# Gates of the first 128 tokens through a DRAM table: GpSimd scatters them, the up projection multiplies them in

## The chip, the cores and the metric

The kernel runs on one core of a Trainium2 chip. Five engines work on their own instruction streams and meet only in semaphores: PE (TensorE, matmuls), DVE (VectorE), ACT (ScalarE), POOL (GpSimd) and SP (SyncE, which here only issues DMAs). Times are microseconds of the device. The metric is the time of one execution, as the median of several runs.

## The reference, cut to what matters

Two blocks are computed one after the other on 256 tokens of 1024 features. The first has a spatial gating, a causal attention of 6 heads, a memory attention of 4 heads and a feed-forward part; the second has a state-space mixer, a convolution mixer and, last, a layer of 16384 small experts. In that last layer each token has 8 heads, and each head picks 16 experts out of 128 x 128 and gives each a gate:

```python
q1, q2 = jnp.split(q, 2, axis=-1)
s1 = jnp.einsum("thd,hkd->thk", q1, sub_keys_1)      # 128 scores per head
s2 = jnp.einsum("thd,hkd->thk", q2, sub_keys_2)
v1, i1 = lax.top_k(s1, 16); v2, i2 = lax.top_k(s2, 16)
cand = (v1[..., :, None] + v2[..., None, :]).reshape(t, 8, 256)
cand_idx = (i1[..., :, None] * 128 + i2[..., None, :]).reshape(t, 8, 256)
top_s, pos = lax.top_k(cand, 16)
expert_idx = jnp.take_along_axis(cand_idx, pos, axis=-1)
gate = jax.nn.softmax(top_s, axis=-1)
act = gelu(jnp.einsum("td,thkd->thk", x, w_down[expert_idx])) * gate
y = jnp.einsum("thk,thkd->td", act, w_up[expert_idx])
```

An expert that two heads of a token pick counts with the sum of its gates.

## The kernel before, in words

The kernel does not fetch single experts. It computes the activation of all 16384 experts for all 256 tokens and multiplies it by a table of gates that is zero where an expert was not picked. Matmuls that need full precision are done as three products of rounded parts: `load_split` loads a weight tile `wf` of 512 KB through SP, ACT rounds it to `wh` (L215), DVE subtracts to get `wl` (L216), and `mm3` (L220 to L222) multiplies. There are 4 buffers of `wf` and 3 of `wh` and `wl`.

Stages, in order of time in the trace of before: first block up to about 330 us, second block's mixers up to about 580 us, then the experts.

- **Mixers of the first block** (up to 120 us): six attention heads (`fox_head`, whose copy out of PSUM is L582) and four memory heads (`mem_head`, L669) run as background work beside projections. After the output projection the pool `ap` is closed and its memory goes to new tiles. Among them is `raw`, which POOL clears in part (L762) and SP then fills with 16 loads (L766); the weights of the feed-forward part stand behind these loads on SP.
- **Selection** (`select(t)`, one pass for each 128 tokens): DVE finds the 16 best of each head, then writes to `sl`, for each of the 128 tokens (partitions) and each of its 128 picks, the two halves i and j of the expert's index (the sums are L1331) and the gate (L1338). The second pass starts when the first is done. PE then transposes `sl` to `pj` (L1342), and ACT copies it to `jt`, in which a column is a token.
- **Down projection** (`for i in range(0, P, 2)`, 128 weight tiles `wd`): 24 matmuls per tile give `S`, expert pairs by 256 tokens; ACT writes its Gelu to the table `AT`, whose row i holds experts (i, j), j on the partitions. `AT` has 96 rows in one tile and 32 in another.
- **Gates** (`gates()`, background of the down projection, after both selections): for each of 256 tokens DVE builds a row of gates by i (`og`, L1407), ACT a row of ones by j (`oh`, L1409 and L1410), and PE multiplies the two (`pg`, L1414) to a table of 128 x 128. Four tokens are one step. Rows of `AT` that are there already are multiplied by `pg` (DVE, L1418); in the others `pg` is stored (ACT, L1421), and the row's Gelu is multiplied in later (ACT to `stage`, L1443; DVE, L1444).
- **Up projection** (`for i in range(P)`, 128 weight tiles `wu`): row i of `AT` is split to `ah` (ACT, L346) and `al` (DVE, L347), and 12 matmuls (L1470) add its product with `wu[i]` to four banks `acc`.

Background work is a generator that yields an estimated cost; `bg.run(budget)` after each weight tile lets it run on until the budget is used up. `BUDGET["select"]` holds until the first gates are there, `BUDGET["down"]` after it. The scheduler orders instructions by program order and priority; what is wrapped in `pin` keeps program order.

Of the kernel before, what the change touches and what calls it, by code (L numbers as in the profile page):

```python
# [16 lines left out]
P = 128  # L17
T = 256
# [17 lines left out]
for _n, _w in _ROWS:  # L36
# [9 lines left out]
    qk=1.5, kv=7.03, u=2.75, wo=2.51, diag=2.05,  # L46
    conf_c=0.995, xbc_c=1.4, conv=1.0,
    z=3.3, z_b=0.867, dt_wait=0.0575, ln_wait=6.66, wo2=3.32, wo2_b=5.58, gn_b=0.1,
    q=0.772, q_b=1.27, select=1.21, down=1.87,
)  # L50
FFN_WAIT, MIX_WAIT = 4.5, 5.5

# [104 lines left out]
def tile_two_blocks(ctx: ExitStack, tc: tile.TileContext, A, out):  # L157
# [172 lines left out]
    def pin(ins):  # L330
        tc.keep_in_program_order(ins)
# [210 lines left out]
    def softmax_t(name, sc, widths, addend):  # L542
# [20 lines left out]
            nc.tensor.transpose(sc[:, i * P:(i + 1) * P], S[:, i * P:(i + 1) * P], ident)  # L563
        yield 0.3

    pofs = {}

    def fox_head(h):
        hp, j = h // 2, h % 2
        pr = slice(64 * j, 64 * j + 64)  # L570
        while f"R{h}" not in done:
            yield None
        sc = bank(f"scf{h}")
        nc.tensor.matmul(sc[:, 0:P], qk[pr, hp, 0:P], qk[pr, 3 + hp, 0:P], start=True, stop=True,
                         skip_group_check=True)
        nc.tensor.matmul(sc[:, P:384], qk[pr, hp, P:T], qk[pr, 3 + hp, :], start=True, stop=True,
                         skip_group_check=True)
        yield 0.2
        yield from softmax_t(f"f{h}", sc, (P, T), R[:, h, :])

        PT = tp.tile([P, 512], F32, tag="PT", name=f"PTf{h}", bufs=3)
        nc.scalar.copy(PT[:, :384], sc[:, :384])  # L582
        yield 0.3
        if hp not in pofs:
            pofs[hp] = bank(f"pof{hp}")
        po = pofs[hp]
        nc.tensor.matmul(po[pr, 0:T], fv[:, 0, h * 64:h * 64 + 64], PT[:, 0:T], start=True, stop=False,
                         skip_group_check=True)
        nc.tensor.matmul(po[pr, P:T], fv[:, 1, h * 64:h * 64 + 64], PT[:, T:384], start=False, stop=True,
                         skip_group_check=True)  # L590
        yield 0.2
        split_to(oh[pr, 3 + hp, :], ol[pr, 3 + hp, :], po[pr, :T])
        yield 0.4
# [63 lines left out]
    def mem_head(h):  # L657
        hp, j = h // 2, h % 2
        pr = slice(64 * j, 64 * j + 64)
        sc = bank(f"scm{h}")  # L660
        for t in range(2):
            nc.tensor.matmul(sc[:, t * T:(t + 1) * T], qk[pr, 6 + hp, t * P:(t + 1) * P], kmT[pr, hp, :],
                             start=True, stop=True, skip_group_check=True)
        yield 0.2
        yield from softmax_t(f"m{h}", sc, (T, T), None)

        PT = tp.tile([P, 512], F32, tag="PT", name=f"PTm{h}", bufs=3)
        PT = PT.rearrange("p (m t) -> p m t", m=2)
        nc.scalar.copy(PT.rearrange("p m (t c) -> p t m c", t=2), sc.rearrange("p (t m c) -> p t m c", t=2, m=2))  # L669
        yield 0.3  # L670
        if hp not in poms:
            poms[hp] = bank(f"pom{hp}")
        po = poms[hp]
        for m in range(2):
            nc.tensor.matmul(po[pr, :T], vm[:, m, h * 64:h * 64 + 64], PT[:, m, :], start=(m == 0), stop=(m == 1),
                             skip_group_check=True)
        yield 0.2
        split_to(oh[pr, 6 + hp, :], ol[pr, 6 + hp, :], po[pr, :T])
        yield 0.4
# [30 lines left out]
    def add_normed(bs, gain, src, dst, eps, name, pool, tmp, then):  # L710

        with tc.high_priority(offset=PRIO):
# [27 lines left out]
                    then(m - 1)  # L740
            then(7)

    x1 = xp.tile([P, 8, T], F32, name="x1", tag="x1")
    h2h, h2l = act_pair("h2", T)
    add_normed(bs, "post_mix", x0, x1, eps1, "pm", xp, tp,
# [553 lines left out]

    ready = dict(q=0)  # L1300

    def select(t):
        for h in range(8):
            while ready["q"] < h // 2 + 1:
# [32 lines left out]
        nc.vector.reciprocal(zs, zs)  # L1337
        nc.vector.tensor_mul(g3, g3, zs.unsqueeze(2).to_broadcast([P, 8, 16]))  # L1338
        yield 0.8
        pj = bank(f"pj{t}")  # L1340
        for i in range(3):
            nc.tensor.transpose(pj[:, i * P:(i + 1) * P], sl[:, i, :], ident)  # L1342
# [33 lines left out]
    sq1.close()  # L1376
    small = resid.tile([P, 8 * T], F32, name="small", tag="x2")
    jt = small[:, 0:3 * T].rearrange("p (i t) -> p i t", i=3)
    ready["q"] = 8
    stage = [small[:, 3 * T + i * 512:3 * T + (i + 1) * 512] for i in range(2)]  # L1380

# [3 lines left out]
    atp = sat.enter_context(tc.tile_pool(name="atp", bufs=1))  # L1385
    AT0 = atp.tile([P, NA, T], F32, name="AT0")
    parts = [(0, NA, AT0)]
    state = dict(rows=0, toks=0)

    def at_rows(a, b):  # L1390
        for lo, hi, t in parts:
# [6 lines left out]
    def gates():  # L1398
        t = p1.tile([P, P - NA, T], F32, tag="at1", name="AT1")
        parts.append((NA, P, t))  # L1400
        for b in range(T // NB):
            t0 = b * NB
            oh = gp.tile([P, NB, P], F32, tag="oh", name=f"oh{b}")
            og = gp.tile([P, NB, P], F32, tag="og", name=f"og{b}")
            for i in range(NB):
# [22 lines left out]
    for i in range(0, P, 2):  # L1428
        S = bank(f"S{i}").rearrange("p (a t) -> p a t", a=2)
        for e in range(2):  # L1430
            wh, wl = load_split(A["wd"][i + e], [P, 8, P])
            for k in range(8):
                mm3(S[:, e, :], wh[:, k, :], wl[:, k, :], xth[:, k, :], xtl[:, k, :], k == 0 and e == 0, k == 7)
            bg.run(BUDGET["select"] if state["toks"] == 0 else BUDGET["down"])
        n = state["toks"]
        rs = list(at_rows(i, i + 2)) if len(parts) > 1 or i < NA else []
        assert len(rs) == 1
        r = rs[0][2]
        if n < T:
            nc.scalar.activation(r[:, :, n:], S[:, :, n:], AF.Gelu)  # L1440
        if n > 0:
            g = stage[(i // 2) % 2].rearrange("p (a t) -> p a t", a=2)
            nc.scalar.activation(g[:, :, :n], S[:, :, :n], AF.Gelu)  # L1443
            nc.vector.tensor_mul(r[:, :, :n], r[:, :, :n], g[:, :, :n])  # L1444
        state["rows"] = i + 2
    bg.drain()

# [3 lines left out]
    late = []  # L1451
    up = gp
    pin(nc.scalar.activation(first, first, AF.Sqrt))
    for i in range(P):
        (_, _, r), = list(at_rows(i, i + 1))
        r = r[:, 0, :]
        if i == NA:

            sat.close()
# [127 lines left out]
```

## Time and profile before

| | |
|---|---|
| median of 3 runs | 1410.69 us (1409.07 to 1411.01) |
| the profiled execution: its time, its span | 1407.69 us, 1406.0 us |
| PE, DVE, ACT, POOL busy | 98%, 72%, 58%, 3% |
| first step of gates, last step, first matmul of the up projection | 828.6, 1037.3, 1042.0 us |

The rows below are of the profiled execution. A row of a group of instructions gives line, engine, operation, written tile, read tiles, shape and count, then busy time and the mean of one in ns, or for one line the shortest, median and longest duration. A row of stretches gives busy time (and count of instructions) of each engine, the clock that TensorE was granted, the busy share of the 16 DMA engines and what they moved. A row in order of time begins with its start, then its duration; in square brackets stands the idle time before it and what ended that. The busy time of PE is modelled: a matmul's row is longer than the distance to the next one, and the distance is what counts.

### The profile page before, as it was taken

To read this page: it belongs to the slowest core of one execution; us is meant where nothing else is said; L and a number is where in the kernel's file an instruction comes from. 1 tells how busy PE (TensorE), PEld (TensorE's weight loads), DVE (VectorE), ACT (ScalarE), POOL (GpSimd) and SP (SyncE) were. 2 spreads that over 40 slices of the span, in tenths; PEclk is the share of its full clock that TensorE was granted. 3 is DMA by queue.
4 is the path that set the end of the run, shared out by engine and by line. 5 is a ranking of instruction groups with operands and counts; after the bars stand their busy time and mean duration, and the time that the engine had idled before them with its cause. 6 is when DMAs were issued, how large, how long until landed. Compare 5 with 4: busy or idle time off the path is not lost.

```text
span 1406.0 us, 26360 instructions
## 1 busy us (share of the span) xinstructions
PE 1384.8 (98%) x10313; PEld 1279.2 (91%) x10313; DVE 1013.7 (72%) x1966; ACT 814.5 (58%) x1431; POOL 43.0 (3%) x64
## 2 busy tenths in 40 slices
PE   9999999999999999999999999999999999999998
PEld 8988999999889899999999999999998888888886
DVE  6886875647557975889799867788875555555654
ACT  6565443435345764645454569999975555555554
POOL 2300000000310000000000000000000000000000
PEclk9999999999999999999999999999999999999999
DMA  8532665654743335446555544444455566656553
GB/s 273 167 91 94 193 194 193 186 175 137 223 137 113 113 121 181 150 150 188 188 180 187 189 165 136 135 136 136 135 172 188 186 188 188 188 192 184 191 185 116
DMA packets 84109, 233.64 MB, mean 166 GB/s; under 512 B 8816, under 2 KB 17904, under 8 KB 83856
## 3 DMA queue, kind: packets, MB, share of 16 engines
q1 hardware_dynamic: 82112, 228.46, 51.4%
q0 software_dynamic: 1296, 2.92, 0.8%
q8 instruction: 81, 1.33, 0.4%
q10 hardware_dynamic: 576, 0.57, 0.1%
q14 instruction: 44, 0.36, 0.1%
HBM read 226.22 MB, written 1.05 MB: 162 GB/s over the span
## 4 chain that ended last, share of the span: by engine, by line
PE 92%; DVE 3%; ACT 2%; DMA 1%; issue 1%; POOL 0%; SPq 0%; ACTq 0%; DVEq 0%
PE acc L1470 25%; PE S L222 9%; PE S L221 9%; PE S L220 9%; PE pg L1414 4%; PE ff L222 4%; PE ff L221 4%; PE ff L220 4%; PE cv L884 2%; PE wo L220 2%; PE wo L222 1%; PE wo L221 1%; PE cf L220 1%; PE q L221 1%; PE cf L222 1%; PE cf L221 1%
## 5 line engine op out<-in xcount | busy, mean ns | idle before, releaser
L216 DVE TENSOR_TENSOR wl<-wf,wh 128x1024 fp32r<-128x1024 f32 (+1 forms) x425 | 515.8, 1215 | 206.1 <-ACT wh L215 205.9
L215 ACT CAST wh<-wf 128x1024 fp32r<-128x1024 f32 (+1 forms) x425 | 441.8, 1040 | 316.1 <-PE S L221 114.6
L220 PE MATMUL S<-xth,wh 128*128 128x256 f32 x1024 | 291.4, 285 | 0.0
L221 PE MATMUL S<-xtl,wh 128*128 128x256 f32 x1024 | 288.4, 282 | 0.0
L222 PE MATMUL S<-xth,wl 128*128 128x256 f32 x1024 | 288.1, 281 | 0.0
L222 PEld LDWEIGHTS S<-xth,wl 128*128 128x128 f32 x1024 | 194.0, 189 | 0.0
L220 PEld LDWEIGHTS S<-xth,wh 128*128 128x128 f32 x1024 | 193.6, 189 | 0.0
L221 PEld LDWEIGHTS S<-xtl,wh 128*128 128x128 f32 x1024 | 192.4, 188 | 0.0
L1470 PE MATMUL acc<-wh,al 128*128 128x512 f32 x512 | 161.4, 395 | 0.0
L1470 PE MATMUL acc<-wl,ah 128*128 128x512 f32 x512 | 161.4, 395 | 0.0
L1470 PE MATMUL acc<-wh,ah 128*128 128x512 f32 x512 | 161.3, 395 | 0.0
L346 ACT CAST ah<-AT 128x256 fp32r<-128x256 f32 x128 | 51.8, 407 | 157.0 <-DVE wl L216 121.1
L1470 PEld LDWEIGHTS acc<-wh,al 128*128 128x128 f32 x512 | 96.0, 187 | 23.5
L1470 PEld LDWEIGHTS acc<-wl,ah 128*128 128x128 f32 x512 | 96.0, 187 | 23.5
L1470 PEld LDWEIGHTS acc<-wh,ah 128*128 128x128 f32 x512 | 95.9, 187 | 23.3
L347 DVE TENSOR_TENSOR al<-AT,ah 128x256 fp32r<-128x256 f32 x128 | 54.1, 425 | 68.7 <-PE acc L1470 67.9
L1409 ACT ACTIVATE oh<-cst,small 128x128 f32<-128x128 f32 x256 | 87.6, 402 | 0.0
L220 PE MATMUL ff<-h2h,wh 128*128 128x256 f32 x256 | 72.0, 282 | 2.3 <-ACT wh L215 2.0
L1407 DVE TENSOR_SCALAR og<-cst,small 128x128 f32<-128x128 f32 x256 | 73.9, 342 | 0.0
L221 PE MATMUL ff<-h2l,wh 128*128 128x256 f32 x256 | 71.6, 280 | 0.1
L222 PE MATMUL ff<-h2h,wl 128*128 128x256 f32 x256 | 70.9, 280 | 0.7 <-DVE wl L216 0.7
L221 PE MATMUL ff<-fal,wh 128*128 128x256 f32 x256 | 71.3, 280 | 0.0
(482 smaller groups left out, 2699.7 us busy)
## 6 DMA issues: line engine op xcount, KB each, us to landing
wf<-in_wd_dram SPq DMA_DIRECT2D x128, 512.0 KB, 3.5
wf<-in_wu_dram SPq DMA_DIRECT2D x128, 512.0 KB, 4.3
wf<-in_w_ff_dram SPq DMA_DIRECT2D x64, 512.0 KB, 3.5
wf<-in_w_out_dram SPq DMA_DIRECT2D x24, 512.0 KB, 3.5
wf<-in_w_conf_dram SPq DMA_DIRECT2D x16, 512.0 KB, 3.9
wf<-in_w_xbc_dram SPq DMA_DIRECT2D x16, 512.0 KB, 3.9
wf<-in_w_q_dram SPq DMA_DIRECT2D x16, 512.0 KB, 3.7
wf<-in_w_fm_dram SPq DMA_DIRECT2D x8, 512.0 KB, 4.7
```

The costliest lines, as they stand in the source:

```text
L215: nc.scalar.copy(wh[:, :n], wf[:, :n])
L216: nc.vector.tensor_sub(wl[:, :n], wf[:, :n], wh[:, :n])
L220: nc.tensor.matmul(o, lh, rh, start=start, stop=False, skip_group_check=True)
L221: nc.tensor.matmul(o, lh, rl, start=False, stop=False, skip_group_check=True)
L222: nc.tensor.matmul(o, ll, rh, start=False, stop=stop, skip_group_check=True)
L346: nc.scalar.copy(dh, src)
L347: nc.vector.tensor_sub(dl, src, dh)
L884: nc.tensor.matmul(pcv[32 * g:32 * g + 32, i, :], taps[:, m, g, q, :], r4[:, i, g, 4 * q:4 * q + T], start=(i == 0 and q == 0), stop=(q == ...
L1407: nc.vector.tensor_scalar(og[:, i, :], iota, jt[:, 0, c:c + 1], jt[:, 2, c:c + 1], op0=OP.is_equal, op1=OP.mult)
L1409: nc.scalar.activation(oh[:, i, :], iota, AF.Abs, scale=-1.0, bias=jt[:, 1, c:c + 1])
L1414: nc.tensor.matmul(pg[:, i, :], oh[:, i, :], og[:, i, :], start=True, stop=True, skip_group_check=True)
L1470: nc.tensor.matmul(acc[t][f], l[:, c], w[:, f * 512:(f + 1) * 512], start=False, stop=e, skip_group_check=True)
```

## The change

- Ahead of the six attention heads a table `G0` of 128 x 128 x 128 numbers (8 MB) is declared in DRAM, ordered by i, j and token. After each head's copy out of PSUM, ACT writes a tile `zg` of zeros, and POOL issues one or two DMAs of 512 KB (rows of 512 bytes) that clear a sixteenth of the table each: eight after the attention heads, eight after the memory heads.
- After the selection of the first 128 tokens, `scatter` computes the place (i x 128 + j) x 128 + token of each pick (DVE, three instructions), and POOL issues 128 indirect DMAs, each with one pick of every token (128 numbers of 4 bytes), which add the gates to `G0`. The 16 of one head need not wait for each other; those of the next head wait for them. PE no longer transposes `sl` for these tokens.
- `gates()` runs for tokens 128 to 255 alone: 32 steps for 64. `BUDGET["down"]` goes from 1.87 to 1.05. Columns of tokens 0 to 127 of `AT` hold the bare Gelu.
- In the up projection the gates of the first tokens are read back, `gt`: rows 0 to 6 by three DMAs of POOL ahead of the loop, then four rows of i (256 KB in rows of 512 bytes) by one DMA of SP. DVE multiplies the first half of each row of `AT` by it, ahead of `split_to`.

```diff
-    q=0.772, q_b=1.27, select=1.21, down=1.87,
+    q=0.772, q_b=1.27, select=1.21, down=1.05,
...
+    G0 = tc.dram_tile([P * P * P, 1], F32, name="G0")
+    G0z = G0.rearrange("(p c n) o -> p c (n o)", p=P, c=16)
+    zg = ap.tile([P, 10, P], F32, name="zg")
+    zero_parts = list(range(16))
+    def zero_g(h, n, after):
+        with tc.issue_after(after.ins):
+            nc.scalar.copy(zg[:, h, :], zeros)
+        for _ in range(n):
+            nc.gpsimd.dma_start(G0z[:, zero_parts.pop(), :].rearrange("p (a n) -> p a n", a=8),
+                                zg[:, h, :].unsqueeze(1).to_broadcast([P, 8, P]))
...
-        nc.scalar.copy(PT[:, :384], sc[:, :384])
+        zero_g(h, 2 if h < 2 else 1, nc.scalar.copy(PT[:, :384], sc[:, :384]))
...
-        nc.scalar.copy(PT.rearrange("p m (t c) -> p t m c", t=2), sc.rearrange("p (t m c) -> p t m c", t=2, m=2))
+        zero_g(6 + h, 2, nc.scalar.copy(PT.rearrange("p m (t c) -> p t m c", t=2),
+                                 sc.rearrange("p (t m c) -> p t m c", t=2, m=2)))
...
+    def scatter(sl):
+        e, gv = idx.bitcast(F32), gates0
+        nc.vector.scalar_tensor_tensor(e, sl[:, 0, :], float(P), sl[:, 1, :], op0=OP.mult, op1=OP.add)
+        nc.vector.tensor_scalar(idx, e, float(P), tokc, op0=OP.mult, op1=OP.add)
+        nc.vector.tensor_copy(gv, sl[:, 2, :])
+        for h in range(8):
+            key = f"head{h}"
+            for j in range(16):
+                c = 16 * h + j
+                s = nc.gpsimd.indirect_dma_start(
+                    out=G0, out_offset=bass.IndirectOffsetOnAxis(ap=idx[:, c:c + 1], axis=0),
+                    in_=gv[:, c:c + 1], in_offset=None, compute_op=OP.add)
+                tc.declare_no_dep(s.ins, group=key, reason="the experts of a head differ")
+                tc.add_to_no_dep_group(key, s.ins)
...
+        if t == 0:
+            scatter(sl)
+            return
         pj = bank(f"pj{t}")
...
-        for b in range(T // NB):
-            t0 = b * NB
+        for b in range(P // NB):
+            t0 = P + b * NB
...
+    G0r = G0.rearrange("(i j t) o -> j i (t o)", i=P, j=P)
+    ga = p1.tile([P, 2, P], F32, name="ga")
+    gts = {0: jt[:, :, 0:P], 3: small[:, 7 * T:8 * T].rearrange("p (a t) -> p a t", a=2), 5: ga}
+    for i in range(7, P, 4):
+        s = 512 * ((i - 7) // 4 % 2)
+        gts[i] = small[:, s:s + 512].rearrange("p (a t) -> p a t", a=4)
+    for n in (0, 3, 5):
+        nc.gpsimd.dma_start(gts[n], G0r[:, n:n + gts[n].shape[1], :])
     for i in range(P):
...
+        if i in gts:
+            n0, gt = i, gts[i][:, :min(P - i, gts[i].shape[1]), :]
+            if i >= 7:
+                pin(nc.sync.dma_start(gt, G0r[:, i:i + gt.shape[1], :]))
+        pin(nc.vector.tensor_mul(r[:, :P], r[:, :P], gt[:, i - n0, :]))
```

Where instructions stand is shown at two places. The first is POOL's stream around the clearing of `raw`, between the first block's mixers and its feed-forward part; of before:

```order
L273 TENSOR_TENSOR rc_mem<-sd_mem,cst 128x2
L602 DMA bsb<-in_bs_dram 64x128 x6
L604 DMA ws<-in_wsT_dram 128x768
L605 AFFINE_SELECT ws<-ws 128x768
L762 MEMSET raw 128x4x4
L273 TENSOR_TENSOR rc_meta<-sd_meta,cst 16x1
```

and of the change:

```order
L617 DMA bsb<-in_bs_dram 64x128 x6
L619 DMA ws<-in_wsT_dram 128x768
L620 AFFINE_SELECT ws<-ws 128x768
L578 DMA G_627<-zg 128x8x128 x16
L779 MEMSET raw 128x4x4
L273 TENSOR_TENSOR rc_meta<-sd_meta,cst 16x1
```

The 16 DMAs that clear `G0` stand ahead of the memset of `raw` (now L779). The memset, and SP's first load of `raw` behind it, now also wait for the landing of the last eight of them. At the end of POOL's stream, which ended with the `rc` of the selection's norm, 128 indirect DMAs and three loads of gates are added.

The second place is DVE's stream at the passage from the down to the up projection (`wl_12831` and `wl_12853` of before, `wl_12413` and `wl_12436` of the change are the first two tiles of `wu`); of before:

```order
L216 TENSOR_TENSOR wl_12853<-wf_12851,wh_12852 128x1024
L1418 TENSOR_TENSOR AT_7310<-AT_7310,pg_12781 128x96x4
L1418 TENSOR_TENSOR AT_9847<-AT_9847,pg_12781 128x30x4
L347 TENSOR_TENSOR al_12826<-AT_7310,ah_12825 128x256
L347 TENSOR_TENSOR al_12848<-AT_7310,ah_12847 128x256
L216 TENSOR_TENSOR wl_12875<-wf_12873,wh_12874 128x1024
L1444 TENSOR_TENSOR AT_9847<-AT_9847,small 128x512
L347 TENSOR_TENSOR al_12870<-AT_7310,ah_12869 128x256
L216 TENSOR_TENSOR wl_12897<-wf_12895,wh_12896 128x1024
```

and of the change:

```order
L216 TENSOR_TENSOR wl_12413<-wf_12411,wh_12412 128x1024
L1488 TENSOR_TENSOR AT_9974<-AT_9974,small 128x2x128
L1514 TENSOR_TENSOR AT_7343<-AT_7343,small 128x128
L216 TENSOR_TENSOR wl_12436<-wf_12434,wh_12435 128x1024
L1514 TENSOR_TENSOR AT_7343<-AT_7343,small 128x128
L216 TENSOR_TENSOR wl_12459<-wf_12457,wh_12458 128x1024
L1488 TENSOR_TENSOR AT_9974<-AT_9974,small 128x2x128
L1514 TENSOR_TENSOR AT_7343<-AT_7343,small 128x128 x2
L347 TENSOR_TENSOR al_12408<-AT_7343,ah_12407 128x256
L347 TENSOR_TENSOR al_12431<-AT_7343,ah_12430 128x256
L347 TENSOR_TENSOR al_12454<-AT_7343,ah_12453 128x256
L216 TENSOR_TENSOR wl_12482<-wf_12480,wh_12481 128x1024
```

The first product of gates and activations (L1514) stands between the `wl` of the first and of the second `wu` tile and waits for POOL's first read-back of `G0`, which waits for all scatters. No step of `pg` stands here any more: on PE the last one is now 8 weight tiles ahead of the end of the down projection, where before it stood one tile ahead. Further on in the up projection DVE's order per row is `al` of a row, `wl` of the next, and then L1514 of the row after that.

## Rows read from the trace of the kernel before

**Rows 1.** The page: busy time of the engines
```profile
PE 1384.8 (98%) x10313; PEld 1279.2 (91%) x10313; DVE 1013.7 (72%) x1966; ACT 814.5 (58%) x1431; POOL 43.0 (3%) x64
```

**Rows 2.** Stretches of selection, of gates and of the up projection
```profile
core 0: us, PE busy (x) PEld busy (x) DVE busy (x) ACT busy (x) POOL busy (x), PEclk, DMA share, GB/s
700.00:750.00 50.00, 50.00 (x425) 50.00 (x424) 47.38 (x148) 27.05 (x38) 0.00 (x0) 1.00 0.54 180
850.00:900.00 50.00, 50.00 (x432) 50.00 (x431) 38.70 (x94) 47.80 (x132) 0.00 (x0) 1.00 0.42 133
1050.00:1100.00 50.00, 50.00 (x216) 40.18 (x215) 29.42 (x36) 26.11 (x36) 0.00 (x0) 1.00 0.60 192
```

**Rows 3.** Chain of waits, 700 to 1060 us
```profile
by line: PE S L222 26.5%; PE S L221 26.3%; PE S L220 26.1%; PE pg L1414 15.8%; PE acc L1470 5.1%; PE pj L1342 0.2%
...
828.60 0.89 PE pg L1414 x8
...
1037.34 1.78 PE pg L1414 x16
1041.97 18.19 PE acc L1470 x78
```

**Rows 4.** Matmuls of the gates
```profile
L1414 PE MATMUL pg<-og,oh x512: 270/275/275, 828.4 to 1038.9; 128*128 128x128 f32 x171
```

**Rows 5.** Transposes of the two selections
```profile
L1342 PE MATMUL pj<-cst,scr x6: 272/273/273, 705.6 to 825.5; 128*128 128x128 f32 x6
```

**Rows 6.** POOL's DMAs of 64 rows of 1136 bytes
```profile
L873 POOL DMA_DIRECT2D r<-h x32: 533/533/602, 351.4 to 397.0; - x32
...
DMA to landing us min/median/max: 2.1/3.5/5.2
```

**Rows 7.** POOL's DMA of 128 rows of 3072 bytes
```profile
L604 POOL DMA_DIRECT2D ws<-in_wsT_dram x1 | 0.6, 597 | 0.0
```

**Rows 8.** Copies of the attention heads out of PSUM
```profile
L582 ACT COPY PTf<-scf x6: 457/474/481, 74.3 to 86.2; 128x384 f32<-128x384 f32 x6
```

**Rows 9.** Copies of the memory heads out of PSUM
```profile
L669 ACT COPY PTm<-scm x4: 586/590/603, 106.0 to 110.6; 128x512 f32<-128x512 f32 x4
```

**Rows 10.** SP's DMA queue, 137 to 146 us: packets, MB, share
```profile
q1 hardware_dynamic: 720, 0.47, 23.0%
```

**Rows 11.** SP's DMA queue, 1100 to 1300 us
```profile
q1 hardware_dynamic: 10245, 37.27, 59.3%
```

**Rows 12.** Stretches of the heads and of the output projection's end
```profile
75.00:107.00 32.00, 32.00 (x271) 28.83 (x269) 28.32 (x73) 20.41 (x52) 0.00 (x0) 1.00 0.33 98
107.00:137.00 30.00, 27.28 (x202) 24.78 (x201) 16.79 (x36) 16.21 (x30) 0.09 (x1) 0.94 0.28 90
```

**Rows 13.** POOL in order of time: the memset of raw
```profile
136.91 0.11 POOL L762 MEMSET raw<- 128x16 f32 x1 [72.05 <-ACT wh L215]
```

**Rows 14.** SP's issues in order of time
```profile
137.04 8.42 SPq L766 DMA_DIRECT2D raw<-in_cols_dram  x16
145.58 28.74 SPq L210 DMA_DIRECT2D wf<-in_w_ff_dram  x13
```

**Rows 15.** Chain of waits, 104 to 175 us
```profile
146.08 4.61 DMA wf<-in_w_ff_dram
```

**Rows 16.** DVE in order of time: last sum of the first selection
```profile
694.53 1.22 DVE L1331 TENSOR_REDUCE scr<-scr 128x64 f32<-128x1024 f32 x1
```

**Rows 17.** DVE in the up projection, in order of time
```profile
1120.46 0.42 DVE L347 TENSOR_TENSOR al<-AT,ah 128x256 fp32r<-128x256 f32 x1 [0.56 <-PE acc L1470]
1121.47 1.23 DVE L216 TENSOR_TENSOR wl<-wf,wh 128x1024 fp32r<-128x1024 f32 x1 [0.58 <-ACT wh L215]
1123.26 0.42 DVE L347 TENSOR_TENSOR al<-AT,ah 128x256 fp32r<-128x256 f32 x1 [0.56 <-PE acc L1470]
```

**Rows 18.** DVE: a product of two 128x128 tiles
```profile
L1338 DVE TENSOR_TENSOR scr<-scr x2: 285/288/292, 663.8 to 783.8; 128x128 f32<-128x128 f32 x2
```

More of the change, by code (lines that the diff above doesn't have):

```diff
@@ L741, in add_normed @@
             then(7)
+    assert not zero_parts
     x1 = xp.tile([P, 8, T], F32, name="x1", tag="x1")
@@ L1378, in tile_two_blocks @@
     jt = small[:, 0:3 * T].rearrange("p (i t) -> p i t", i=3)
+    idx = small[:, 7 * T:7 * T + P].bitcast(U32)
+    gates0 = small[:, 7 * T + P:8 * T]
+    tokc = resid.tile([P, 1], F32, name="tokc", tag="tokc")
+    nc.vector.tensor_mul(idx.bitcast(F32), ident, iota)
+    nc.vector.reduce_sum(tokc, idx.bitcast(F32), axis=AX.X)
     ready["q"] = 8
@@ L1387, in tile_two_blocks @@
     parts = [(0, NA, AT0)]
-    state = dict(rows=0, toks=0)
+    state = dict(rows=0, toks=P)
     def at_rows(a, b):
@@ L1433, in tile_two_blocks @@
                 mm3(S[:, e, :], wh[:, k, :], wl[:, k, :], xth[:, k, :], xtl[:, k, :], k == 0 and e == 0, k == 7)
-            bg.run(BUDGET["select"] if state["toks"] == 0 else BUDGET["down"])
+            bg.run(BUDGET["select"] if state["toks"] == P else BUDGET["down"])
         n = state["toks"]
@@ L1438, in tile_two_blocks @@
         r = rs[0][2]
-        if n < T:
-            nc.scalar.activation(r[:, :, n:], S[:, :, n:], AF.Gelu)
-        if n > 0:
+        if n == P:
+            nc.scalar.activation(r, S, AF.Gelu)
+        else:
+            nc.scalar.activation(r[:, :, :P], S[:, :, :P], AF.Gelu)
+            if n < T:
+                nc.scalar.activation(r[:, :, n:], S[:, :, n:], AF.Gelu)
             g = stage[(i // 2) % 2].rearrange("p (a t) -> p a t", a=2)
-            nc.scalar.activation(g[:, :, :n], S[:, :, :n], AF.Gelu)
-            nc.vector.tensor_mul(r[:, :, :n], r[:, :, :n], g[:, :, :n])
+            nc.scalar.activation(g[:, :, P:n], S[:, :, P:n], AF.Gelu)
+            nc.vector.tensor_mul(r[:, :, P:n], r[:, :, P:n], g[:, :, P:n])
         state["rows"] = i + 2
```

## The prediction

> **What bounds the kernel now.** I read the page first: PE is busy for 98% of the span, DVE for 72%, POOL for 3% [rows 1]. A share over the whole span hides stages, so next the table of stretches: in the selection, in the gates and in the up projection alike PE is busy for all of 50 us, at a granted clock of 1.00 (the upper level, 2.4 GHz), while DVE comes to 47.4 in the selection and ACT to 47.8 in the gates [rows 2]. Since the busy time of PE is modelled, the chain of waits has to confirm it: from 700 to 1060 us every piece of it is a matmul, 15.8% of them the gates' `pg`, and the up projection's first matmul follows the last step of gates without a gap [rows 3]. So a matmul taken out of this stretch shortens the span by its own distance to the next one, until another engine is last.
>
> **Gates on PE: minus 28.8.** A step of four tokens is 8 matmuls, and the chain gives 0.89 us for it [rows 3]; its row says 275 ns for one matmul, but they overlap, so the distance counts. 512 matmuls are 64 steps [rows 4]; 32 go: 32 x 0.89 = 28.5 us. Of six transposes three go [rows 5], at 0.89 / 8 = 0.11 us each 0.3 us. What could be late next is ACT or DVE, but both lose the same 32 steps (`og`, `oh`, the products with `pg`), and 24 matmuls of a weight tile (50 / 425 = 0.118 us each) last 2.8 us, far more than what rounding and subtracting a tile takes there. The last eight tiles run without gates at all. PE stays the bound and the full 28.8 comes through.
>
> **Clearing the table: plus 2.5.** No trace of before shows a POOL DMA of 1024 rows. The two nearest take 533 ns for 64 rows [rows 6] and 597 ns for 128 [rows 7]. A line through them gives 1 ns per row, so 1.5 us; in proportion to rows it would be 8 x 0.597 = 4.8 us. I take 1.5, because the two rows show that most of an issue does not grow with rows. The first eight DMAs can follow the attention heads' copies, from 75 us on [rows 8], the other eight the memory heads', from 106.9 on [rows 9], and the last of these is issued near 119.
> What they move is eight times 1024 rows of 512 bytes. The nearest price by size is SP's queue while it loads `raw`: 23.0% of 16 engines over 9 us are 33 us for 720 packets, 46 ns for one of some 650 bytes [rows 10]; for weights it is 59.3% x 16 x 200 / 10245 = 185 ns for 3640 bytes [rows 11]. Eight DMAs thus take 8192 x 46 / 16 = 23.6 us of all engines; scaled by bytes from the weights' packets 13.3; at a weight packet's full price 95. The engines are also busy with weights for 0.28 x 30 = 8.4 us of that stretch [rows 12]. From 106.9 on this ends at 139 by the first price, with 2 us for landing at 141, and at 131 by the second. What waits for it is POOL's memset of `raw`, in the trace at 136.9 [rows 13]; behind it on SP stand 16 loads of 8.4 us and then weights [rows 14], and the chain of waits runs through the first of those weights, for 4.6 us [rows 15]. So each us late costs a us: 4 by the first price, nothing by the second. 512 bytes lie below the first, so I take 2. The ends are 0 and, at the weights' price, 106.9 + 95 + 8 + 2 - 137 = 75.
> The first eight meet the loads of 75 to 107 us, 23.6 + 0.33 x 32 = 34 us of the engines in 32 [rows 12]; weights are loaded up to four tiles ahead, which covers some us, and PE had no gap there. ACT's ten copies of zeros, a third of a head's copy in columns and thus some 0.3 us each, lie in a stretch where ACT is busy for 20.4 of 32 us; I add 0.5 for both.
>
> **Scatter: nothing, if it is over in time.** It can start when the last sum of the first selection is through, 695.8 [rows 16], and two `wl` and two index instructions behind it, so at 700. The first read-back has to have landed before DVE comes to the product that stands between the first two `wl` of the up projection, some 3 us ahead of its first matmul, now at 1042.0 - 28.8 = 1013. Less 4 us for the read-back (issue and landing [rows 6]), the last scatter must be through by 1006: a window of 306 us. In it lie 128 issues and eight waits for a landing, one behind each head, 3.5 us each [rows 6]: 28 us. So each scatter may take (306 - 28) / 128 = 2.17 us. No row shows an indirect DMA. From below, a plain one of 128 rows is 0.6 us [rows 7], 104 us for all; from above, were each to wait for the one before it, 128 x (0.6 + 3.5) = 525 us. I take 1.2 us, twice the plain issue of the same number of rows, nearer the lower end because those of a head need not wait for each other: 128 x 1.2 + 28 = 182 us, over at 882. Beyond 2.17 each 0.1 us costs 12.8. POOL has nothing else behind the scatters, and the down projection covers them. DVE's five added instructions are about 1.5 us in a stretch where it has 2.6 of 50 us free [rows 2] and PE is tiles ahead; nothing.
>
> One page speaks against this. The rows show POOL's plain DMAs at a steady 533 ns, 602 at most, beside a working DVE [rows 6], but those read no indices. The Trainium skill, SBUF — State Buffer, "Who interferes with whom", says that a DVE instruction with two SBUF inputs and a GpSimd instruction that reads SBUF exclude each other, the later waiting for the whole of the earlier. No run here shows it for a scatter; if it holds for one, the third rival is what follows.
>
> **Up projection: nothing.** DVE gets a product of 128x128 per row, 0.29 us [rows 18], in a period of 2.80 us in which it idles 0.56 us before `al` and 0.58 before `wl` [rows 17]; the product stands right before `al`, inside the first gap. SP gets 31 loads of 512 rows, 512 x 46 / 16 = 1.5 us of the engines in 11.2 us, which lifts their share from 0.60 [rows 2] to 0.73. Each is queued behind the weight load of the row before, four rows ahead of its use. If the gap before `al` were gone, each row would lose up to 0.29 us, 37 in all; the gap is twice the product.
>
> **Sum.** -28.8 + 2.5 = -26.3. The profiled span of 1406.0 becomes 1379.7, its time of 1407.69 becomes 1381.4; the median of the runs stands 3.0 above the profiled execution, so 1384.4.
>
> **Rivals.**
> 1. *The scatter is too slow* (slower than before). If a scatter takes 3.0 us, 128 x 3.0 + 28 = 412, DVE stands at the first product for 106 us and with it everything: 1490. It decides from 2.17 us on, and from 2.38 on it eats the whole gain. For it: adding in DRAM reads and writes, and the upper bound is 4.1. Against: nothing in the order serialises the 16 of a head.
> 2. *Clearing is issued at 4.8 us each*: the first eight keep POOL until 75 + 38 = 113, the second eight until 151, landing at 153, 16 late: 1384.4 + 16 - 2 = 1398. For it: the two rows span only 64 rows.
> 3. *Each scatter waits for a subtraction of DVE*, 1.23 us [rows 17]: 128 x 2.43 + 28 = 339 us, 33 late: 1417, slightly slower. Against: DVE subtracts for only 1.2 of each 2.8 us, and half the wait fits into the window.
> 4. *Weights come late under the scatter*: 128 packets at 46 ns are 0.37 us of 16 engines per 1.2 us, 0.31 on top of 0.54 [rows 2]. The engines hold out on average, but single tiles may be late: 5 to 15 us, about 1394.
> That the steps of gates don't go is excluded by the order, which has 32.
>
> **How the numbers follow.** My forecast has 0.63 (1379 to 1391 by its own costs), rival 1 0.10, rival 2 0.13, rival 3 0.04, rival 4 0.07; 0.03 stays for something else. A measurement here tells 0.2%, 2.8 us, from no change. The forecast and rivals 2 and 4 are faster: 0.83. Rivals 1 and 3 are slower: 0.14. The rest is 0.03. The range goes from 1378, a little below a clearing that costs nothing, to 1402, behind rival 2; rivals 1 and 3 and worse forms of the others are left out.
>
> **What would show it.** `pg` halves to 256 matmuls, and the up projection begins near 1016. POOL's row of indirect DMAs has a mean below 2.17 us and its last one ends well before 1000; if DVE's first product there shows an idle time put down to a DMA, rival 1 or 3 is true. The memset of `raw` starts before 141; if it starts near 153, rival 2. The period of the up projection stays at 2.80 us. The prediction is wrong if PE gets gaps in the down projection, or if the first matmul of the up projection waits.

## The result, and the profile after

The changed kernel takes 1375.79 us (median of four runs, 1375.08 to 1377.82) against 1410.85 for the kernel before (four runs, 1409.07 to 1415.57). The ratio is 0.9749, 95% interval 0.9723 to 0.9775: 35.1 us less. The forecast was 1384.4, its range began at 1378, so the direction was right and the gain 8.6 us larger than forecast, outside the range. The profiled execution took 1376.38 us, its span is 1374.7.

The busy time of the engines, from the page of the changed kernel [rows 1]:

```profile
PE 1347.8 (98%) x10054; PEld 1251.3 (91%) x10054; DVE 985.5 (72%) x1920; ACT 754.2 (55%) x1261; POOL 301.4 (22%) x211
```

The three stretches in the changed kernel [rows 2]:

```profile
core 0: us, PE busy (x) PEld busy (x) DVE busy (x) ACT busy (x) POOL busy (x), PEclk, DMA share, GB/s
700.00:750.00 50.00, 50.00 (x425) 50.00 (x425) 45.01 (x130) 22.62 (x27) 43.00 (x24) 1.00 0.80 187
850.00:900.00 50.00, 50.00 (x430) 50.00 (x429) 32.75 (x70) 39.95 (x103) 42.86 (x24) 1.00 0.66 149
1050.00:1100.00 50.00, 50.00 (x223) 41.39 (x222) 33.80 (x56) 27.18 (x37) 0.00 (x0) 1.00 0.68 212
```

PE is still busy throughout, and POOL now for 43 of 50 us. The last row is the surprise: 223 matmuls of the up projection in 50 us where there were 216, at the same granted clock. The rows of `pg`, of the transposes and of the last product of the down projection, in the changed kernel (count: shortest/median/longest ns, first and last start) [rows 4, 5]:

```profile
L1455 PE MATMUL pg<-og,oh x256: 271/275/377, 830.3 to 991.7; 128*128 128x128 f32 x128
...
L1378 PE MATMUL pj<-cst,scr x3: 272/272/272, 826.3 to 826.5; 128*128 128x128 f32 x3
...
L222 PE MATMUL S<-xth,wl x1024: 274/282/287, 622.1 to 1014.4; 128*128 128x256 f32 x171
```

The same row of the kernel before:

```profile
L222 PE MATMUL S<-xth,wl x1024: 279/282/286, 620.7 to 1041.7; 128*128 128x256 f32 x171
```

Half of `pg` and of the transposes is gone, and this stage, from the first start of its last product's row to the last, takes 392.3 us in place of 421.0: 28.7 less, where the sum had 28.8. GpSimd's part, POOL in order of time and its row of scatters [rows 6, 7, 13]:

```profile
107.87 7.03 POOL L578 DMA_DIRECT2D G<-zg  x8 [18.83 <-ACT zg L576]
137.50 0.11 POOL L779 MEMSET raw<- 128x16 f32 x1 [22.60 <-ACT wh L215]
...
L1329 POOL DMA_INDIRECT G<-small x128: 1540/1675/2691, 699.1 to 978.1; - x128
```

A clearing DMA takes 7.03 / 8 = 0.88 us to issue, and `raw` is set at 137.50, 0.6 us later than before. A scatter takes 1.54 to 2.69 us, and the last begins at 978.1.

Between the two projections stands something that the kernel before did not have: PE and then ACT in order of time around it (start, duration, in brackets the idle time before and its releaser):

```profile
1018.06 1.22 PE L1528 MATMUL acc<-wh,ah 128*128 128x512 f32 x2 [3.38 <-ACT ah L346]
```

```profile
1014.60 1.04 ACT L215 CAST wh<-wf 128x1024 fp32r<-128x1024 f32 x1 [1.79 <-PE S L221]
1015.55 0.38 ACT L1483 ACTIVATE AT<-S 128x256 f32<-128x256 f32 x1
1015.83 0.38 ACT L1487 ACTIVATE small<-S 128x256 f32<-128x256 f32 x1
1016.22 1.28 ACT L1497 ACT_TABLE_LOAD   x1
1017.51 0.20 ACT L1497 ACTIVATE first<-first 128x1 f32<-128x1 f32 x1
1017.62 0.69 ACT L346 CAST ah<-AT 128x256 fp32r<-128x256 f32 x2
```

PE waits 3.38 us for `ah` of row 0, and ACT comes to it only after the Gelu of the last tile and a load of the Sqrt table. The stretches behind the gap (PE busy, granted clock, DMA share):

```profile
1015.00:1020.00 5.00, 1.94 (x5) 0.79 0.94 318
1020.00:1025.00 5.00, 5.00 (x21) 0.87 0.16 49
1025.00:1030.00 5.00, 5.00 (x24) 1.00 0.54 158
```

Behind the gap the granted clock falls to the lower level (1.2 GHz) for a while, which costs (0.21 + 0.13) x 5 = 1.7 us of work. So the change first lost some 5 us that the forecast doesn't have, and gained still more somewhere else: the pace of matmuls whose instructions the change does not touch.

### The profile page after: what moved, and what is told of

Read it like the earlier page. It is cut to its first block, busy times and chain, and to the rows that moved or that the text cites. A ratio compares the mean times of both kernels' runs of the same rounds, so it can differ in the third digit from the quotient of the medians.

```text
span 1374.7 us, 25834 instructions
## 1 busy us (share of the span) xinstructions
PE 1347.8 (98%) x10054; PEld 1251.3 (91%) x10054; DVE 985.5 (72%) x1920; ACT 754.2 (55%) x1261; POOL 301.4 (22%) x211
## 4 chain that ended last, share of the span: by engine, by line
PE 92%; DVE 3%; ACT 2%; issue 1%; DMA 0%; POOL 0%; DVEq 0%; ACTq 0%; SPq 0%
PE acc L1528 25%; PE S L222 9%; PE S L221 9%; PE S L220 9%; PE ff L222 4%; PE ff L220 4%; PE ff L221 4%; PE pg L1455 2%; PE cv L901 2%; PE wo L220 2%; PE wo L222 2%; PE wo L221 2%; PE cf L220 1%; PE q L221 1%; PE cf L222 1%; PE cf L221 1%
## 5 line engine op out<-in xcount | busy, mean ns | idle before, releaser
L1329 POOL DMA_INDIRECT G<-small x128 | 241.9, 1890 | 163.2 <-DVE small L1323 124.5
L1528 PE MATMUL acc<-wl,ah 128*128 128x512 f32 x512 | 158.6, 390 | 0.0
L1528 PE MATMUL acc<-wh,al 128*128 128x512 f32 x512 | 158.5, 390 | 0.0
L222 PE MATMUL ff<-fah,wl 128*128 128x256 f32 x256 | 69.6, 277 | 0.3 <-DVE wl L216 0.3
```

The lines of the kernel that those rows point to most:

```text
L222: nc.tensor.matmul(o, ll, rh, start=False, stop=stop, skip_group_check=True)
L1329: s = nc.gpsimd.indirect_dma_start(out=G0, out_offset=bass.IndirectOffsetOnAxis(ap=idx[:, c:c + 1], axis=0), in_=gv[:, c:c + 1], in_offset ...
L1528: nc.tensor.matmul(acc[t][f], l[:, c], w[:, f * 512:(f + 1) * 512], start=False, stop=e, skip_group_check=True)
```

## The experiments

The first question is why the up projection runs faster. A row of it is 12 matmuls with `wh` and `wl` streamed (moving) and `ah`, `al` loaded (stationary). By start times a row takes 2.80 us before and 2.72 after; the counts of 216 and 223 in 50 us also hold one or two matmuls begun ahead of the stretch. Between the two programs the matmuls of this stage differ in nothing but addresses: the change allocates `tokc`, the numbers of the tokens, 4 bytes a partition that take up 32, in the pool `resid` (a line that the shortened diff leaves out), and the tiles allocated behind it in SBUF stand 32 bytes higher. By the allocation in the built programs the first `ah` is at 88864, not 88832: in steps of 256 bytes all `ah` and `al` are at 32 in place of 0, the weights at 32 in both. The rival is the new product of DVE, which moves the splitting in time.

**The shift alone, in the kernel before.**

```
     small = resid.tile([P, 8 * T], F32, name="small", tag="x2")
+    tokc = resid.tile([P, 1], F32, name="tokc", tag="tokc")
+    nc.vector.memset(tokc, 0.0)
```

> The kernel before with one unused tile of 32 bytes a partition (`tokc`, cleared once) in the pool `resid`, so that every tile allocated behind it stands 32 bytes higher, as in the changed kernel; nothing else. Theory A (place): the up projection is faster in the changed kernel because `ah` and `al` stand 32 bytes higher. Then its period falls from 2.80 to 2.72 us, 128 x 0.08 = 10 us, and with the second feed-forward product, whose matmuls are 113 instead of 117 ns apart in the changed kernel (768 x 4 ns = 3 us), less 1 us for the queries (120 instead of 117), the time is about 1398, 13 below before. Theory B (product): the extra product of DVE moves the splitting of the activations to a time that suits PE better. Then the period stays at 2.80 and the time within 3 us of before.

Measured 1399.35 us against 1410.65, ratio 0.9914 (0.9898 to 0.9931). A stretch of its up projection:

```profile
1100.00:1150.00 50.00, 50.00 (x223) 1.00 0.63 195
```

32 unused bytes are worth 11.3 us (theory A). No product, scatter or table is in this kernel.

**The change without the shift.**

```
-    tokc = resid.tile([P, 1], F32, name="tokc", tag="tokc")
+    tokc = resid.tile([P, 8], F32, name="tokc", tag="fs")[:, 0:1]
```

> The changed kernel with `tokc` put into the buffer that `fs` uses at the end, so that no tile behind it is shifted by 32 bytes; the same instructions otherwise. Theory A (place): the period of the up projection goes back to 2.80 us and the time to about 1388 (1376 + 10 + 3 - 1), which is what the scatter alone is worth. Theory B (product): the period stays at 2.72 and the time at 1376.

Measured 1390.35 us against 1410.65, ratio 0.9855 (0.9839 to 0.9872):

```profile
1100.00:1150.00 50.00, 50.00 (x216) 1.00 0.70 215
```

The period is back at 2.80 (theory A). The change by what it is meant to do is worth 20.3 us, not 35. The two parts, 11.3 and 20.3, come to 31.6, 3.5 short of the 35.1; the intervals, some 2.3 us to either side for each part and 3.7 for the whole, leave room for that.

**The change without the products.**

```
-        pin(nc.vector.tensor_mul(r[:, :P], r[:, :P], gt[:, i - n0, :]))
```

> The changed kernel without DVE's 128 products of the up projection: the table is still cleared, scattered into and read back, but the first 128 tokens are not multiplied by their gates. Theory A (place): the period stays at 2.72 us and the time within 3 us of 1376. Theory B (product): the period goes back to 2.80, the time to about 1386.

Measured 1372.53 us, ratio to before 0.9721 (0.9705 to 0.9737). A stretch of its up projection:

```profile
1050.00:1100.00 50.00, 50.00 (x222) 1.00 0.69 212
```

The pace stays, and theory B falls. This run also says where the gap comes from, since it has none (it is 3.3 us below the changed kernel); its first matmul of the up projection:

```profile
1020.17 0.62 PE L1527 MATMUL acc<-wh,ah 128*128 128x512 f32 x2
```

**All places of `ah` and `al`, in the kernel before.**

```
-        ah = up.tile([P, T], F32R, tag="oh", name=f"ah{i}")
-        al = up.tile([P, T], F32R, tag="og", name=f"al{i}")
+        o = 8 * (i // 8)
+        ah = up.tile([P, T + 128], F32R, tag="oh", name=f"ah{i}")[:, o:o + T]
+        al = up.tile([P, T + 128], F32R, tag="og", name=f"al{i}")[:, o:o + T]
```

> The kernel before, where `ah` and `al` of the up projection begin 0, 32, 64 ... 480 bytes into a larger buffer, each offset for 8 consecutive rows; the same instructions otherwise. Theory A: the distance of two matmuls depends on the offset: 233 ns for rows 0 to 7 (offset 0), 227 ns for rows 8 to 15 (offset 32), and each of the other offsets has one constant value of its own, the pattern being that of their distance from the place of `wh` and `wl`. Theory B: 233 ns at every offset.

The period, from the first and last start of the 96 matmuls of each 8 rows (times 12/95); `ah` begins at a multiple of 256 bytes for the offset 0, the weights 32 bytes behind one:

| offset, bytes | 0, 256 | 32, 288 | 64, 320 | 96, 352 | 128, 384 | 160, 416 | 192, 448 | 224, 480 |
|---|---|---|---|---|---|---|---|---|
| period, us | 2.80 | 2.72 | 2.80 | 2.80 | 2.81 | 2.79 | 2.80 | 2.75 |

The same from stretches of 20 us at the offsets 32, 64 and 128 (2.72 us a row are 88.2 matmuls in 20 us, 2.80 are 85.7; the view also counts those begun before):

```profile
1069.00:1089.00 20.00, 20.00 (x90) 1.00 0.64 187
1091.00:1111.00 20.00, 20.00 (x88) 1.00 0.63 188
1136.00:1156.00 20.00, 20.00 (x87) 1.00 0.62 185
```

The run as a whole, one execution, took 1410.07 us. The period hangs on the offset, and it repeats after 256 bytes: only 32 and 224 are clearly faster than the rest. The best is where `ah` and the weights have the same place in 256 bytes. Is it that, or the place of `ah` itself?

**The weights' place, `wh` alone.**

```
-        wh = wpool.tile([P, 1024], F32R, tag="wh", name=f"wh{cnt[0]}")
+        wh = wpool.tile([P, 1088], F32R, tag="wh", name=f"wh{cnt[0]}")[:, o:o + 1024]
...
-            wh, wl = load_split(A["wd"][i + e], [P, 8, P])
+            wh, wl = load_split(A["wd"][i + e], [P, 8, P], 8 * (i // 16))
...
-        wh, wl = load_split(A["wu"][i], [P, D])
+        wh, wl = load_split(A["wu"][i], [P, D], 8 * (i // 16))
```

> The kernel before, where the rounded weights `wh` of the down and of the up projection begin 0, 32, 64 ... 224 bytes into a larger buffer, each offset for 16 consecutive rows; `wl`, `ah` and `al` stay (`ah` and `al` at 0 in steps of 256 bytes, `wl` at 32). Theory A1 (what counts is the place of the stationary `ah` against that of the streamed weights): matmuls that stream `wh` are 227 ns apart at the offset 224, where `wh` stands at 0 as `ah` does, and 233 at the offset 0; those that stream `wl` stay at 233. Theory A2 (the place of `ah` alone counts): 233 ns at every offset.

Measured 1412.16 us, one execution. Stretches of 40 us at the offsets 0 and 224:

```profile
1050.00:1090.00 40.00, 40.00 (x173) 1.00 0.63 196
1358.00:1398.00 40.00, 40.00 (x175) 1.00 0.52 159
```

Neither theory held. By start times the period of the up projection is 2.80 us at the offset 0, 2.77 at 224, between them at the others. The place of `wh` matters, against A2, but a matmul that streams `wh` from the place of `ah` is not simply 227 ns from the next: those with `ah` took 227 to 231, and with other offsets some that stream the unmoved `wl` took 227. So the pace isn't a sum over single matmuls.

**Weights and activations together, at 0.**

```
+    wpad = wpool.tile([P, 56], F32, tag="wpad", name="wpad", bufs=1)
+    nc.vector.memset(wpad, 0.0)
...
+    gpad = gp.tile([P, 8], F32, tag="gpad", name="gpad", bufs=1)
+    nc.vector.memset(gpad, 0.0)
```

> The kernel before with two unused tiles, cleared once: 224 bytes at the head of the pool of the weights and 32 at the head of the pool that holds `ah` and `al`. `wh` and `wl` so stand at 0 in steps of 256 bytes, and `ah` and `al` at 0 as well; in the changed kernel all of them stand at 32, in the kernel before the weights at 32 and `ah` and `al` at 0. Theory A1 (the place of `ah` and `al` against the streamed weights counts): the period of the up projection is 2.72 us and the time about 1400. Theory A2 (the place of `ah` and `al` themselves counts): 2.80, about 1410.

Measured 1400.48 us against 1411.91, ratio 0.9923 (0.9896 to 0.9949):

```profile
1100.00:1150.00 50.00, 50.00 (x223) 1.00 0.66 192
```

`ah` stands where it stands in the kernel before, at 0, and the stage is fast: the places against each other count (A1), when all the streamed tiles share it.

**The gap: rows 0 and 1 split early.** (`split_row` is the product and the split of one row, `read_back` the three first loads from the table.)

```
+        if i == P - 2:
+            read_back()
+            for q in range(2):
+                split[q] = split_row(q, AT0[:, q, :], gts[0][:, q, :], gp)
         if n == P:
             nc.scalar.activation(r, S, AF.Gelu)
```

> The changed kernel, where the read-back of the table and the products and splitting of the first two rows (`ah`, `al` of rows 0 and 1) are written ahead of the Gelu of the last tile of the down projection, in place of behind it and behind ACT's load of the Sqrt table. Theory A (order on ACT): PE stands for 3.4 us ahead of the up projection because `ah` of row 0 is queued on ACT behind that Gelu and the table load; so the up projection begins at about 1014.5 in place of 1018.1, the stretch at the lower clock behind the gap goes too (3.4 us at half speed, 1.7 us), and the time is about 1371. Theory B (something else is late there, the read-back or the weights): the gap stays and the time is 1376.

```profile
1016.57 0.62 PE L1544 MATMUL acc<-wh,ah 128*128 128x512 f32 x2
```

No idle time stands before it, and the granted clock is 1.00 from 1010 to 1040: the gap was the order on ACT. From the first matmul of the down projection (623.8 us here, 621.7 in the changed kernel) to this one it is 3.6 us less than in the changed kernel. The time is 1374.05 us (1370.35 to 1375.62), ratio to before 0.9731 (0.9706 to 0.9756), 3 us above what theory A gave. The ranges of this and of the changed kernel overlap, so the 5 us are shown in the trace and not in the median.

**No table at all.**

```
-        nc.gpsimd.dma_start(gts[n], G0r[:, n:n + gts[n].shape[1], :])
...
-                pin(nc.sync.dma_start(gt, G0r[:, i:i + gt.shape[1], :]))
-        pin(nc.vector.tensor_mul(r[:, :P], r[:, :P], gt[:, i - n0, :]))
+        pin(nc.vector.tensor_mul(r[:, :P], r[:, :P], iota[:, :P]))
```

and neither the clearing nor the 128 scatters are issued (POOL clears `ga` instead).

> The changed kernel without the table: no clearing, no scatter, no read-back; the products of the first 128 tokens stay but multiply by a constant, so their gates are left out. It is the bound that the change could reach if the table cost nothing. Theory A (the table is hidden: 0.6 us at the memset of `raw`, nothing elsewhere): 1374 to 1376. Theory B (the table's transfers and the locking of POOL and DVE cost several us somewhere): 1370 or less.

```profile
1018.49 1.22 PE L1511 MATMUL acc<-wh,ah 128*128 128x512 f32 x2 [3.38 <-ACT ah L346]
```

Measured 1375.32 us, 0.5 from the changed kernel, ratio to before 0.974 (0.9722 to 0.9758). Clearing, scatter and read-back together cost nothing that can be measured (theory A). The gap is there without a read-back and is gone without the products: it is the products, held in order, that move `ah` behind the Gelu and the table load.

**32 scatters more.**

```
+        for j in range(32):
+            s = nc.gpsimd.indirect_dma_start(
+                out=G0, out_offset=bass.IndirectOffsetOnAxis(ap=idx[:, j:j + 1], axis=0),
+                in_=tokz, in_offset=None, compute_op=OP.add)
...
```

(`tokz` is a column of zeros in the tile of `tokc`.)

> The changed kernel with 32 more scatters, which add zeros to entries of the table, behind the 128. At 2.2 us each they are over 70 us later, at about 1050 in place of 980, and the read-back at 1055, 44 us behind the place where DVE reaches the first product (1011). Theory A (a window, and beyond it each us of scatter costs a us): about 1376 + 44 = 1420. Theory B (there is slack that the trace doesn't show, or what stands behind the product catches up): below 1400.

Measured 1414.15 us (ratio to before 1.0007, 0.9992 to 1.0022), 38 above the changed kernel. DVE at its first product, PE at its first matmul of the up projection, and POOL shortly before:

```profile
1054.39 0.29 DVE L1522 TENSOR_TENSOR AT<-AT,small 128x128 f32<-128x128 f32 x1 [39.37 <-DMA small<-G]
```

```profile
1058.18 1.22 PE L1536 MATMUL acc<-wh,ah 128*128 128x512 f32 x2 [40.05 <-ACT ah L346]
```

```profile
1029.32 1.54 POOL L1335 DMA_INDIRECT G<-tokc,small  x1 [0.30 <-issue]
```

Theory A, in this one step: DVE stands for 39.4 us, and the run is 38 longer. 44 was too much; once DVE stands still, the scatters come every 1.84 us, not 2.2. In the changed kernel the last scatter is over at 980, the read-back some 5 us later, and DVE comes to its first product without a wait at 1011:

```profile
1011.48 0.28 DVE L1514 TENSOR_TENSOR AT<-AT,small 128x128 f32<-128x128 f32 x1
```

So the gates' gain hangs on a margin of some 25 us of POOL.

**The place of the other streams.** If places matter so much in the up projection, they may in the down projection. On top of the early split:

```
-        h = act.tile([P, 8, TM], F32R, name=f"{name}h", tag="acth")
-        l = act.tile([P, 8, TM], F32R, name=f"{name}l", tag="actl")
-        return h[:, :, :t], l[:, :, :t]
+        h = act.tile([P, 8 * TM], F32R, name=f"{name}h", tag="acth")
+        l = act.tile([P, 8 * TM], F32R, name=f"{name}l", tag="actl")
+        o = 48 if t == T else 0
+        return [v[:, o:o + 8 * t].rearrange("p (k t) -> p k t", k=8) for v in (h, l)]
```

> The changed kernel with the early splitting of rows 0 and 1 (as in the run of that name), and the activations of the pool `act` (`xth`, `xtl`, `h2h`, `os1h` and the like, with 256 tokens) laid 192 bytes higher in their buffers and their 8 blocks 1024 bytes apart in place of 1088, so that each block stands at 224 in steps of 256 bytes, where the second feed-forward product and the output projection of the changed kernel stream theirs at 113 ns a matmul. Theory A (place): the 3072 matmuls of the down projection come to 113 to 114 ns in place of 118.7, 15 us, and the first feed-forward product and the queries of attention give 4 more: about 1374 - 19 = 1355. Theory C (the place of a stream counts only in the form of those two products, since blocks of the down projection that stand at 224 now take 118 as the others do): 1370 to 1374.

Measured 1364.13 us, ratio to before 0.968 (0.9641 to 0.972). The second stretch lies in the selection, the first in the feed-forward:

```profile
200.00:300.00 100.00, 100.00 (x851) 1.00 0.63 185
700.00:750.00 50.00, 50.00 (x443) 1.00 0.79 183
```

443 matmuls in 50 us in place of 425: the place counts in the down projection too, against theory C. From its first matmul to the up projection's first, it takes 11.4 us less than in the run with the early split, where theory A had 15, and the time is 9 us above theory A's. The feed-forward lost: 851 in 100 us, where the changed kernel has 869. Its second product, whose own tiles were not moved, slowed from 113 to 117 ns by start times. Its row here:

```profile
L222 PE MATMUL ff<-fah,wl x256: 276/281/387, 159.9 to 318.6; 128*128 128x256 f32 x128
```

**The same, with `h2h` and `h2l` at their old places.**

```
+        if t == TM or name == "h2":
+            return [v.rearrange("p (k t) -> p k t", k=8)[:, :, :t] for v in (h, l)]
```

> The run before this one (activations at 224), with `h2h` and `h2l` alone back at their old places (first block at 32, blocks 1088 bytes apart). There the second feed-forward product took 117 to 118 ns a matmul, though its own operands stand where they take 113 to 114 in the changed kernel. Theory A3 (the pace belongs to the whole stream of matmuls: those of the first product, which run between them, set it too): the second product goes back to 114, 768 x 3.8 = 3 us, and the time to about 1361. Theory A4 (something else differs there, such as where the stream is in time): it stays at 117 to 118 and the time at 1364.

```profile
200.00:300.00 100.00, 100.00 (x868) 100.00 (x868) 62.02 (x67) 44.35 (x48) 0.00 (x0) 1.00 0.64 190
700.00:750.00 50.00, 50.00 (x444) 50.00 (x443) 48.38 (x150) 23.40 (x27) 43.30 (x23) 1.00 0.81 189
```

```profile
L222 PE MATMUL ff<-fah,wl x256: 276/276/385, 159.5 to 315.2; 128*128 128x256 f32 x128
```

Measured 1360.69 us (1357.62 to 1362.48), ratio to before 0.964 (0.9624 to 0.9656): A3, and the fastest of all, 15 us below the changed kernel without an instruction less. In the selection DVE is now busy for 48.4 of 50 us, so by this share little more is to be had there.

## Why the prediction was wrong

**The step that failed** is "Up projection: nothing" and in it "The period of the up projection stays at 2.80 us". The period fell to 2.72, 128 x 0.08 = 10.2 us. The reasoning about DVE's product was sound (it costs the period nothing; the run without products has the same pace), but it took for granted that a matmul whose instructions are unchanged keeps its pace. The two runs on the shift settle it: the shift alone gives 11.3 us, the change without it 20.3. Without the shift the same change takes 1390.35 us, inside the stated range and 6 above the forecast, about what the transition below cost. The second feed-forward product gained by the same shift. Its row in the changed kernel, and below it the row of before:

```profile
L222 PE MATMUL ff<-fah,wl x256: 276/276/385, 158.3 to 314.0; 128*128 128x256 f32 x128
```

```profile
L222 PE MATMUL ff<-fah,wl x256: 277/280/388, 157.9 to 316.3; 128*128 128x256 f32 x128
```

It lasts 155.7 us in place of 158.4, 2.7 less.

**Gates, minus 28.8:** right, 28.7 by the stage's length.

**Clearing, plus 2.5:** too high. An issue took 0.88 us, where I took 1.5, and the packets were other than I thought. GpSimd's queue from 105 to 137 us (packets, MB, share of 16 engines):

```profile
q0 software_dynamic: 1152, 4.19, 40.6%
```

The eight DMAs went as 1024 packets of 4096 bytes (and 128 of 4), not as 8192 of 512, and 40.6% of 32 us is 13.0 us of all engines, not 23.6: the lowest of my estimates, 13.3, was nearly right. The last packet ended at 127.6, ten us ahead of the memset of `raw` at 137.50, which the profile puts down to ACT, as before. Its 0.6 us are not shown to be the clearing's: the memset started at 137.88 in the kernel before with the shift alone, and at 135.82 in the run without a table. Rival 2 is out.

**Scatter, nothing:** right in what it cost, wrong in its size. I took 1.2 us each; the distance from scatter to scatter is (978.1 - 699.1) / 127 = 2.20 us, 1.89 busy and 0.30 between two. By my own limit of 2.17 it should have been late; it was not, because the 28 us for eight waits for a landing did not come (no idle time of POOL within the scatters is longer than 0.31 us). Over at 980 in place of 882, it used most of the window that the sum gave it. Rival 1 was nearer than the 0.10 that I gave it. Rival 4 is out: in the selection the 16 DMA engines are busy for 0.80 in place of 0.54, and PE does 425 matmuls in 50 us as before.

**Rival 3** has the right mechanism and too high a price. POOL and DVE from the first selection's end on:

```profile
714.84 1.81 POOL L1329 DMA_INDIRECT G<-small  x1 [0.30 <-issue]
716.96 2.40 POOL L1329 DMA_INDIRECT G<-small  x1 [0.30 <-issue]
719.66 1.54 POOL L1329 DMA_INDIRECT G<-small  x1 [0.30 <-issue]
721.51 1.54 POOL L1329 DMA_INDIRECT G<-small  x1 [0.30 <-issue]
```

```profile
716.73 1.21 DVE L216 TENSOR_TENSOR wl<-wf,wh 128x1024 fp32r<-128x1024 f32 x1
...
720.04 1.21 DVE L216 TENSOR_TENSOR wl<-wf,wh 128x1024 fp32r<-128x1024 f32 x1
```

The scatter at 716.96 begins inside a subtraction that ends at 717.94, 0.98 us later, and takes 0.86 longer than 1.54; the one at 719.66 begins before a subtraction and takes 1.54. Of 128 scatters 70 begin inside a subtraction of `wl` and have a mean of 2.15 us, the other 58 one of 1.58; in the run with 32 more, where DVE stands still, all those begun from 1016 on are at 1.54. For nearly all of the 70 the time above 1.54 is what is left of the subtraction at the scatter's start, less 0.13 us. This agrees with the Trainium skill, SBUF — State Buffer, "Who interferes with whom", so far as the scatter is the later of the two: it waits for what is left of the subtraction. On average that was 0.35 us a scatter, 45 in all, not 1.23 for each. DVE did not wait the other way: subtractions that begin within a scatter take 1.23 us at most, as without one. There the page, by which the later waits whichever it is, and this trace differ, and the measurement decides. Five of the clearing DMAs, which read no indices, began inside a subtraction too, and took 0.88 to 0.89 us as the others did.

**The transition** is a term that I did not have. I named a first matmul that waits as what would make the prediction wrong, and it waited: 3.4 us, and 1.7 for the lower clock behind it. I had looked for what covers PE in numbers of matmuls and not at ACT's order, where the program shows `ah` of row 0 behind the table load. It is luck that this loss, which I left out, took back some 40% of the 12.9 us that I also left out (10.2 and 2.7).

**The sum by what was measured:** gates -28.7, clearing +0.6 at most, transition +5.1, up projection -10.2, feed-forward -2.7, together -35.9, against -35.1 by the medians and -31.3 between the profiled executions. The 3.0 us that I added between profile and median did not come: the changed kernel's profiled execution lies 0.6 above its median. The profiled execution of before spent less time at the lower clock: a mean of 0.997 over 1406 us loses some 4 us, one of 0.993 over 1375 some 10, and only 1.7 of the difference are behind the gap. So the two profiles differ by some 4 us less than the sum. Nor is the sum exact: for the two parts by themselves it has -23.0 and -12.9, where the runs on the shift gave -20.3 and -11.3.

## What to carry to other kernels

A tile of a few bytes moves everything allocated behind it, and here the place of a matmul's operands against each other, in steps of 256 bytes, was worth 3 to 4% of the pace of a PE-bound stage: compare the addresses of two builds before explaining a gain by the instructions, and try a few paddings, which here cost some bytes and no time that showed. Work that goes to an idle engine was free here as long as its window held, so work out how far it is from the end of the window and which other engine can hold it up. Where something is held in order ahead of a handover between stages, read the orders of all the engines there, ACT's table loads included.

## What the runs showed of the hardware

- Matmuls of 512 columns followed each other at 227 or 233 ns at a granted clock of 1.00, those of 256 columns at 113 to 120, with nothing changed but the places of operands. In the up projection the pattern repeats after 256 bytes. What rule gives it stays open: of the places that ran, equal ones were best in the up projection (at 32 and at 0), while the second feed-forward product and the down projection were best with the moving tiles at 224 and the weights at 32, and a stream's pace also hung on the matmuls interleaved with it.
- An indirect DMA of 128 single elements that adds into DRAM took POOL 1.54 us plus 0.30 until the next, and longer when it began inside a subtraction of DVE with two SBUF inputs: by what was left of it, less 0.13 us. A plain one of 512 KB, which went as 128 packets of 4096 bytes, took 0.88, inside a subtraction too.
